# A two-layer hybrid decoder on one core: index scores of all blocks first, three selections side by side, and only the low halves of weights stored ahead

## The chip, the cores and the metric

The kernel runs on 1 core of one Trainium2 chip. Its engines are TensorE (PE, matmuls; its weight loads are listed as PEld), VectorE (DVE), ScalarE (ACT), GpSimd (POOL) and SyncE (SP, which issues most DMAs). Each works through a queue of its own in order. The metric is the device time of one execution in microseconds; lower is better.

## The reference, cut to what matters

Sequence 512, width 1024, two layers. Each layer projects the normed input once and splits it among four mixers, then does cross-attention and a gated FFN of width 2816. The change touches the second mixer, whose queries see only 256 keys each (here min(256, 512/4) = 128), chosen by an index score:

```python
def dsa_mixer(cols, pos, ...):
    ...
    topk = min(DSA_TOPK_MAX, l_ // 4)
    def block(bi):                      # 128 queries each, 4 blocks
        ...
        rel = jax.nn.relu(jnp.einsum('bthd,bsd->bhts', iqb, ik))       # 8 index heads
        score = jnp.einsum('bhts,bth->bts', rel, iwb).astype(F32)
        score = jnp.where(causal[None], score, -jnp.inf)
        _, idx = lax.top_k(score, topk)
        ...                             # attention over the chosen keys
```

The other mixers are hgrn2 (a gated linear recurrence), nsa (compressed, selected and window attention) and mlstm. The rest of a layer is `x + mixed @ w_out`, cross-attention on 256 memory rows, and `x + (silu(a) * b) @ w2` with `a, b = split(h @ w13)`.

## The kernel before

**Weights in two halves.** Matmuls keep near-float32 precision by splitting every operand into a high half (rounded by a copy) and a low half (the rest): three matmuls per product. `weight_tile` loads a raw tile (`wr`, 3 buffers; 6 in the later stages of a layer), makes the high half on ACT (`wh`, L292) and the low half on POOL (`wl`, L293); `wh` and `wl` have 6 buffers each. A typical tile is 128 x 512, 256 KB.

**Split ahead.** During layer 0's FFN, `split_ahead` does this for the 72 tiles of layer 1's first stage, in the order of the list `FIRST`: load (`pr`, 2 buffers), copy on ACT (L317), subtraction on POOL (L318), both halves written to DRAM in one transfer (`phl`, 2 buffers, L320). In layer 1 `split_tile` loads both halves from there and neither ACT nor POOL works on them. `ffn` puts `NSPLIT` = 3 such pieces into the program after each of its 22 chunks and one after every second of its 16 output columns (`fo`); the pieces left over then go into the second half's columns.

**The first stage of a layer** weaves several generators: a generator yields costs, and `mix` takes next the one that is least far along its planned total. On one side runs `dsa` (the index branch, planned total 74), then `hg_space`, which closes the index pool and opens the pool of `h_v` and `h_g` in its place. On the other side (225) run nsa's projections and its attention, mlstm's projections and its four heads, and the remaining projections (`ml_in2`, `dsa_in2`, `hg_in`). The last two of these, `hgi` and `hgg` for `h_v` and `h_g`, stand behind `hg_space`. A scheduler then orders each engine's queue at build time, by this program order and by what is ready in its own model of time; weight loads and splits are moved ahead (`first`).

**The index branch before.** For each block tb = 1, 2, 3 in turn (n = 256, 384, 512 keys; block 0 needs none): `index(tb)` splits the queries, transposes them (PE, then ACT to `iqT`), and for each of 8 heads does one matmul into one PSUM bank (`dt`), a relu on ACT (`rel`, 4 buffers) and a multiply-add into the score `iacc` on DVE. Then `select(tb)` finds the 128 largest scores of each row in 16 rounds of `max` (8 values, L696) and `match_replace` (L697; in the trace a value load and the replacement), and turns what was replaced into the mask `dmask` (L700). All blocks share one `iacc`, so the three selections run one after another.

**After the first stage** come hgrn2 with the attention of dsa and two thirds of the output projection (`hg`, `dsa_attn`, `out_stage`), then cross-attention, then the FFN. Layer 0's first stage ends near 277 us, its FFN runs from 494 to 864, layer 1's first stage from there to 1114, its FFN from 1326 to the end.

Of the kernel before, what the change touches and what calls it, by code (L numbers as in the profile page):

```python
# [21 lines left out]
NEG = -1e30  # L22
# [172 lines left out]


RAWS = 6
NSPLIT = 3

FIRST = ["dsai", "nsa0", "nsa1", "nsaT", "ml1", "mlT0", "mlT2", "cw", "ml0", "mlT1", "mlT3", "dsaq", "ckv", "hgT0", "hgT2",  # L200
         "hgT1", "hgT3", "hgi", "hgg"]
# [5 lines left out]
class Kernel:  # L207
# [73 lines left out]
    def weight_tile(self, tile, pool=None):  # L281

        nc = self.nc
        if tile in self.pre:
            return self.split_tile(tile)
        raw = self.raw_tile(tile)
        _, nk, c = tile
        kw = {"bufs": KC} if pool else {}
        hi = (pool or self.wp).tile([128, nk, c], FR, name="wh", tag="wh", **kw)
        lo = (pool or self.wp).tile([128, nk, c], FR, name="wl", tag="wl", **kw)  # L290
        with ExitStack() if pool else self.first():
            nc.scalar.activation(hi, raw, AF.Copy)  # L292
            nc.gpsimd.tensor_tensor(lo, raw, hi.bitcast(FT), op=OP.subtract)  # L293
        return [(hi[:, k], lo[:, k]) for k in range(nk)]

    def split_tile(self, tile):

        _, nk, c = tile
        both = []
        for j, n in enumerate(("wh", "wl")):  # L300
            w = self.wp.tile([128, nk, c], FR, name=n, tag=n)
            with self.first():
                self.nc.sync.dma_start(w.rearrange("p a b -> p (a b)").bitcast(FT), self.pre[tile][:, j])
            both.append(w)
        return [(both[0][:, k], both[1][:, k]) for k in range(nk)]

    def split_ahead(self, pool, l):

        nc, src = self.nc, self.i["wst"]
        for key in FIRST:  # L310
            for tile in self.plans[l][key]:
                off, nk, c = tile
                n = nk * c
                raw = pool.tile([128, n], FT, name="pr", tag="pr", bufs=2)
                nc.sync.dma_start(raw, bass.AP(tensor=src.tensor, offset=src.offset + off, ap=[[n, 128], [1, n]]))
                both = pool.tile([128, 2, n], FR, name="phl", tag="phl", bufs=2)
                nc.scalar.activation(both[:, 0], raw, AF.Copy)  # L317
                nc.gpsimd.tensor_tensor(both[:, 1], raw, both[:, 0].bitcast(FT), op=OP.subtract)  # L318
                d = self.tc.dram_tile([128, 2, n], FT, name=f"whl{off}")
                nc.sync.dma_start(d, both.bitcast(FT))  # L320
                self.pre[tile] = d
                yield

# [318 lines left out]
    def dsa(self, pool, keep):  # L642
        nc = self.nc
        idx = self.d_idx
        st = self.t(pool, "d_st", [128, 64], bufs=1)

        ik = idx[:, :, 256:288]
        self.sumsq(st[:, 4:8], ik, pool)
        self.rsqrt(pool, st[:, 8:12], st[:, 4:8], 1.0 / 32, EPS)
        self.tt(ik, ik, st[:, 8:12, None].to_broadcast([128, TB, 32]), OP.mult)  # L650
        self.tt(ik, ik, self.row("idxk_gain")[:, None, :].to_broadcast([128, TB, 32]), OP.mult)
        self.rope(idx[:, :, 256:288].rearrange("p t (h d) -> p t h d", h=1), self.ic, self.isn, 4, pool)
        iq = idx[:, :, 0:256].rearrange("p t (h d) -> p t h d", h=8)
        self.rope(iq, self.ic, self.isn, 4, pool)
        iks = self.t2(pool, "iks", [128, TB, 96], FR)
        nc.vector.tensor_copy(iks[:, :, 0:32], ik)
        nc.vector.tensor_copy(iks[:, :, 32:64], ik)
        self.tt(iks[:, :, 64:96], ik, iks[:, :, 0:32].bitcast(FT), OP.subtract)
        ikT = self.t(pool, "ikT", [128, S], FR, bufs=1)
        self.transpose_blocks(ikT[0:96], lambda j: iks[:, j, :].bitcast(FT), TB, nc.vector.tensor_copy, rows=96,  # L660
                              pool=pool)

        yield 4.0

        def index(tb):
            n = (tb + 1) * 128
            iqs = self.t(pool, "iqs", [128, 8, 96], FR, bufs=1)
            nc.scalar.activation(iqs[:, :, 0:32], iq[:, tb], AF.Copy)
            nc.scalar.activation(iqs[:, :, 64:96], iq[:, tb], AF.Copy)
            self.tt(iqs[:, :, 32:64], iq[:, tb], iqs[:, :, 0:32].bitcast(FT), OP.subtract, nc.gpsimd)  # L670
            iqT = self.t(pool, "iqT", [128, 8, 128], FR, bufs=1)
            for g in range(2):
                self.transpose_blocks(iqT[0:96, 4 * g:4 * g + 4].rearrange("p a b -> p (a b)"),
                                      lambda j: iqs[:, 4 * g + j, :].bitcast(FT), 4, self.act_copy, rows=96,
                                      pool=pool)
            acc = self.t(pool, "iacc", [128, S], bufs=1)[:, :n]
            for h in range(8):
                sc = self.psum("sc", pool=pool)
                nc.tensor.matmul(sc[:, :n], iqT[0:96, h], ikT[0:96, :n], start=True, stop=True)
                rel = self.t2(pool, "rel", [128, S])  # L680
                nc.scalar.activation(rel[:, :n], sc[:, :n], AF.Relu, scale=1.0 / 16)
                w = idx[:, tb, 288 + h:289 + h]
                if h == 0:
                    nc.vector.tensor_scalar(acc[:, :n - 128], rel[:, :n - 128], w, None, op0=OP.mult)
                    nc.vector.scalar_tensor_tensor(acc[:, n - 128:n], rel[:, n - 128:n], w, self.k("neg"),
                                                   op0=OP.mult, op1=OP.add)
                else:
                    nc.vector.scalar_tensor_tensor(acc, rel[:, :n], w, acc, op0=OP.mult, op1=OP.add)
                yield 0.7
            return acc  # L690

        def select(tb, acc, masks):
            n = (tb + 1) * 128
            m8 = self.t(pool, "m8", [128, 8])
            for r in range(16):
                nc.vector.max(m8, acc)  # L696
                nc.vector.match_replace(acc, m8, acc, -3e38)  # L697
                yield 0.4 + 0.25 * tb
            masks[tb] = self.t(keep, f"dmask{tb}", [128, n], BF, bufs=1)
            nc.vector.tensor_scalar(masks[tb], acc, -2e38, NEG, op0=OP.is_gt, op1=OP.mult)  # L700

        masks = self.d_masks = {0: None}
        for tb in range(1, TB):
            acc = yield from index(tb)
            yield from select(tb, acc, masks)

    def dsa_attn(self, pool):
        nc, l = self.nc, self.l
# [758 lines left out]
    def ffn(self, pool):  # L1467
        nc = self.nc
# [4 lines left out]
        ahead_of = lambda n: [next(ahead, None) for j in range(n)]  # L1473
        for g in range(2):
            gs = []
            for c in range(g * FFG, g * FFG + FFG):
                a = self.psum("acc")
                self.mm_T(a, self.weights(f"ffa{c}"), self.x)
                b = self.psum("sc")
# [13 lines left out]
                gs.append((gh, gl))  # L1493
                ahead_of(NSPLIT)
            for c in range(KC):
                acc = self.psum("acc")
                self.mm_T(acc, self.weights(f"fo{g}_{c}"), gs)
                if c % 2 == 0:
                    ahead_of(1)
                self.residual(c, acc)  # L1500
                if g == 1 and last_layer:
                    nc.sync.dma_start(self.o["y"][c * 128:c * 128 + 128, :], self.xT[c])
                elif g == 1:
                    self.square_sum(c)
# [32 lines left out]
    def run(self):  # L1537
        nc = self.nc
        late = ExitStack()
        for l in range(DEPTH):  # L1540
# [8 lines left out]
            right, index = ExitStack(), ExitStack()  # L1549
            self.hqf = self.pool(right, "hgqf", side="right")  # L1550
            self.mo = {2: self.t(self.mp, "mo2", [128, 2, S], bufs=1), 3: self.t(self.mp, "mo3", [128, TB, 256], bufs=1)}
            pd = self.pool(index, "dsa", n2=4, n4=0, side="right")
            self.alias[id(pd)] = {"tp": "dt", "sc": "dt"}
            acc = self.dsa_in(pd)
            if l == 0:
# [32 lines left out]
            ph = self.pool(left, "hg", n2=2, n4=0)  # L1588
# [11 lines left out]
            with ExitStack() as e:  # L1600
                p = self.pool(e, "xa")
# [29 lines left out]
```

## Time and profile before

| | us |
|---|---|
| median of 3 runs | 1687.93 |
| lowest, highest | 1684.38, 1699.76 |
| the profiled execution | 1688.9 |
| its span, first to last instruction | 1687.1 |
| its mean granted TensorE clock | 0.972 |

The profile is of one execution; times in it are microseconds from the span's start. The granted clock is given as a share of TensorE's full speed. An idle engine costs nothing unless another waits for it.

### The profile page before, as it was taken

Reading aid. Unit: us, or ns where it says so; the run is one execution under the profiler, and the core shown is the slowest. Engines: PE = TensorE matmul, PEld = TensorE weight load, DVE = VectorE, ACT = ScalarE, POOL = GpSimd, SP = SyncE. Lnnn points to the kernel's source line nnn. Section 1 sums busy time; section 2 is a strip of 40 time slices with the busy share of each in tenths; the row PEclk is TensorE's granted clock in tenths of the full one; section 3 lists DMA queues with packets and bytes.
Section 4 is the critical chain, followed back from the end, with each engine's and each line's share of the span. In section 5 each row is a group of like instructions: output and inputs, shape, how many; then the busy total and the mean of one; then the engine's idle time right before and its main releaser. Section 6 shows DMA issues by size and latency. Waiting matters only on the chain.

```text
span 1687.1 us, 25484 instructions
## 1 busy us (share of the span) xinstructions
PE 1607.5 (95%) x9256; PEld 1333.1 (79%) x9262; DVE 924.0 (55%) x1760; ACT 712.5 (42%) x1525; POOL 799.1 (47%) x698
## 2 busy tenths in 40 slices
PE   7899998998899989999999999989998999999999
PEld 7778877777788868888898887677877888888887
DVE  5697688876755330344225884879786644123420
ACT  5555453454654443443324433423665433223321
POOL 5664333456448888874412010144672344444442
PEclk9999997999999999999999999979999999999999
DMA  5342212212338999953355734122131233333331
GB/s 160 89 119 76 70 34 84 57 38 85 112 121 286 305 316 319 333 192 93 105 156 178 262 107 132 58 95 57 45 119 38 66 97 90 92 100 94 94 103 66
DMA packets 114365, 212.72 MB, mean 126 GB/s; under 512 B 12984, under 2 KB 30136, under 8 KB 114240
## 3 DMA queue, kind: packets, MB, share of 16 engines
q1 hardware_dynamic: 111888, 206.11, 38.7%
q10 hardware_dynamic: 2032, 3.94, 0.7%
q8 instruction: 73, 1.20, 0.3%
q0 software_dynamic: 320, 1.05, 0.2%
q14 instruction: 52, 0.43, 0.1%
HBM read 170.69 MB, written 40.35 MB: 125 GB/s over the span
## 4 chain that ended last, share of the span: by engine, by line
PE 84%; DVE 8%; issue 3%; DMA 2%; POOL 2%; ACT 2%; SPq 0%; POOLq 0%; ACTq 0%; DVEq 0%
PE acc L329 14%; PE acc L331 14%; PE acc L330 14%; PE sc L330 5%; PE sc L331 5%; PE sc L329 5%; PE acc L339 3%; PE acc L340 3%; PE acc L341 3%; PE hb L856 3%; PE o L574 2%; PE sc L552 2%; PE tp L493 2%; PE mb L1048 1%; PE dt L493 1%
## 5 line engine op out<-in xcount | busy, mean ns | idle before, releaser
L293 POOL TENSOR_TENSOR wl<-wr,wh 128x512 fp32r<-128x512 f32 (+5 forms) x432 | 551.7, 1285 | 459.3 <-ACT wh L292 447.8
L292 ACT ACTIVATE wh<-wr 128x512 fp32r<-128x512 f32 (+5 forms) x432 | 252.1, 592 | 336.2 <-PE acc L330 149.2
L329 PE MATMUL acc<-xh,wh 128*128 128x512 f32 (+1 forms) x704 | 276.9, 395 | 0.8 <-ACT xh L1283 0.5
L330 PE MATMUL acc<-xl,wh 128*128 128x512 f32 (+1 forms) x704 | 274.6, 390 | 2.9 <-DVE xl L1277 2.9
L331 PE MATMUL acc<-xh,wl 128*128 128x512 f32 (+1 forms) x704 | 275.4, 392 | 0.4 <-POOL wl L293 0.4
L466 DVE TENSOR_TENSOR xT<-acc,xT 128x512 f32<-128x512 f32 (+1 forms) x112 | 68.1, 611 | 214.4 <-PE acc L331 213.6
L329 PEld LDWEIGHTS acc<-xh,wh 128*128 128x128 f32 x704 | 133.9, 191 | 32.1 <-issue 1.7
L330 PEld LDWEIGHTS acc<-xl,wh 128*128 128x128 f32 x704 | 134.3, 191 | 30.8 <-DVE xl L1277 4.0
L331 PEld LDWEIGHTS acc<-xh,wl 128*128 128x128 f32 x704 | 134.1, 190 | 28.7 <-POOL wl L293 1.1
L329 PE MATMUL acc<-f_gh,wh 128*128 128x512 f32 x352 | 139.1, 397 | 6.8 <-ACT f_gh L1491 6.8
L339 PE MATMUL acc<-wh,xh 128*128 128x256 f32 (+2 forms) x480 | 140.6, 296 | 4.9 <-DMA wh<-whl 3.8
L331 PE MATMUL acc<-f_gh,wl 128*128 128x512 f32 x352 | 139.7, 398 | 0.7 <-POOL wl L293 0.7
L330 PE MATMUL sc<-xl,wh 128*128 128x512 f32 x352 | 139.7, 397 | 0.0
L330 PE MATMUL acc<-f_gl,wh 128*128 128x512 f32 x352 | 139.5, 398 | 0.0
L340 PE MATMUL acc<-wl,xh 128*128 128x256 f32 (+2 forms) x480 | 139.0, 291 | 0.0
L331 PE MATMUL sc<-xh,wl 128*128 128x512 f32 x352 | 139.0, 395 | 0.0
L329 PE MATMUL sc<-xh,wh 128*128 128x512 f32 x352 | 138.0, 393 | 0.0
L341 PE MATMUL acc<-wh,xl 128*128 128x256 f32 (+2 forms) x480 | 137.4, 288 | 0.0
L318 POOL TENSOR_TENSOR phl<-pr,phl 128x512 fp32r<-128x512 f32 (+3 forms) x72 | 95.1, 1321 | 35.0 <-ACT phl L317 31.8
L317 ACT ACTIVATE phl<-pr 128x512 fp32r<-128x512 f32 (+3 forms) x72 | 44.2, 613 | 133.9 <-DMA pr<-in_wst 117.2
L339 PEld LDWEIGHTS acc<-wh,xh 128*128 128x128 f32 x480 | 92.9, 194 | 8.8 <-DMA wh<-whl 4.3
L340 PEld LDWEIGHTS acc<-wl,xh 128*128 128x128 f32 x480 | 93.3, 195 | 1.4 <-issue 0.8
(407 smaller groups left out, 3159.8 us busy)
## 6 DMA issues: line engine op xcount, KB each, us to landing
wr<-in_wst SPq DMA_DIRECT2D x332, 256.0 KB, 2.7
whl<-phl SPq DMA_DIRECT2D x52, 512.0 KB, 3.9
pr<-in_wst SPq DMA_DIRECT2D x52, 256.0 KB, 4.1
wh<-whl SPq DMA_DIRECT2D x52, 256.0 KB, 4.1
wl<-whl SPq DMA_DIRECT2D x52, 256.0 KB, 4.4
wr<-in_wst SPq DMA_DIRECT2D x48, 128.0 KB, 2.2
wr<-in_wst SPq DMA_DIRECT2D x32, 192.0 KB, 2.4
whl<-phl SPq DMA_DIRECT2D x8, 524.0 KB, 3.7
```

The costliest lines, as they stand in the source:

```text
L292: nc.scalar.activation(hi, raw, AF.Copy)
L293: nc.gpsimd.tensor_tensor(lo, raw, hi.bitcast(FT), op=OP.subtract)
L318: nc.gpsimd.tensor_tensor(both[:, 1], raw, both[:, 0].bitcast(FT), op=OP.subtract)
L329: self.nc.tensor.matmul(acc, wh, xh, start=(j == 0), stop=False)
L330: self.nc.tensor.matmul(acc, wh, xl, start=False, stop=False)
L331: self.nc.tensor.matmul(acc, wl, xh, start=False, stop=(j == n - 1))
L339: self.nc.tensor.matmul(acc, xh[:, s], wh, start=(first and j == 0), stop=False)
L340: self.nc.tensor.matmul(acc, xh[:, s], wl, start=False, stop=False)
L341: self.nc.tensor.matmul(acc, xl[:, s], wh, start=False, stop=(last and j == n - 1))
L466: self.nc.vector.tensor_add(self.xT[c][:, cols], acc, self.xT[c][:, cols])
L493: self.nc.tensor.transpose(p[:rows, j * 128:j * 128 + 128], src(j), self.ident)
L856: nc.tensor.matmul(sc[s0:s1, b + t0:b + t1], kk[po:po + 64, b + s0:b + s1], qq[po:po + 64, b + t0:b + t1], start=True, stop=True)
```

## The change

The index scores of blocks 1 to 3 are all computed first, each into an accumulator of its own (`iacc1` to `iacc3`); queries are split and transposed four heads at a time with two buffers. Then 16 rounds run, and each round does one `max` and one `match_replace` for each of the three blocks. The masks are made at the end. Yielded costs add up to the same totals. The index pool gives one of its four `t2` buffers (among them `rel`) for this. Of the split ahead only the low half is written to DRAM (256 KB per typical tile, was 512); in layer 1 the raw tile is loaded, its high half made on ACT as in layer 0, and the low half loaded where POOL would have made it. `NSPLIT` is 2, and `ffn` puts two pieces after every chunk and every output column.

```diff
-NSPLIT = 3
+NSPLIT = 2
...
     def weight_tile(self, tile, pool=None):
-        if tile in self.pre:
-            return self.split_tile(tile)
         raw = self.raw_tile(tile)
...
             nc.scalar.activation(hi, raw, AF.Copy)
-            nc.gpsimd.tensor_tensor(lo, raw, hi.bitcast(FT), op=OP.subtract)
+            if tile in self.pre:
+                nc.sync.dma_start(lo.rearrange("p a b -> p (a b)").bitcast(FT), self.pre[tile][:, :])
+            else:
+                nc.gpsimd.tensor_tensor(lo, raw, hi.bitcast(FT), op=OP.subtract)
...
     def split_ahead(self, pool, l):
...
-                both = pool.tile([128, 2, n], FR, name="phl", tag="phl", bufs=2)
-                nc.scalar.activation(both[:, 0], raw, AF.Copy)
-                nc.gpsimd.tensor_tensor(both[:, 1], raw, both[:, 0].bitcast(FT), op=OP.subtract)
-                d = self.tc.dram_tile([128, 2, n], FT, name=f"whl{off}")
-                nc.sync.dma_start(d, both.bitcast(FT))
+                hi = pool.tile([128, n], FR, name="ph", tag="ph", bufs=2)
+                lo = pool.tile([128, n], FR, name="pl", tag="pl", bufs=2)
+                nc.scalar.activation(hi, raw, AF.Copy)
+                nc.gpsimd.tensor_tensor(lo, raw, hi.bitcast(FT), op=OP.subtract)
+                d = self.tc.dram_tile([128, n], FT, name=f"wl{off}")
+                nc.sync.dma_start(d, lo.bitcast(FT))
...
+        accs = {tb: self.t(pool, f"iacc{tb}", [128, (tb + 1) * 128], bufs=1) for tb in range(1, TB)}
...
-            iqT = self.t(pool, "iqT", [128, 8, 128], FR, bufs=1)
+                iqT = self.t(pool, "iqT", [128, 4, 128], FR, bufs=2)
...
+        for tb in range(1, TB):
+            yield from index(tb)
+
+        for r in range(16):
+            for tb in range(1, TB):
+                m8 = self.t(pool, f"m8{tb}", [128, 8])
+                nc.vector.max(m8, accs[tb])
+                nc.vector.match_replace(accs[tb], m8, accs[tb], -3e38)
                 yield 0.4 + 0.25 * tb
-            masks[tb] = self.t(keep, f"dmask{tb}", [128, n], BF, bufs=1)
-            nc.vector.tensor_scalar(masks[tb], acc, -2e38, NEG, op0=OP.is_gt, op1=OP.mult)
-
         masks = self.d_masks = {0: None}
         for tb in range(1, TB):
-            acc = yield from index(tb)
-            yield from select(tb, acc, masks)
+            masks[tb] = self.t(keep, f"dmask{tb}", [128, (tb + 1) * 128], BF, bufs=1)
+            nc.vector.tensor_scalar(masks[tb], accs[tb], -2e38, NEG, op0=OP.is_gt, op1=OP.mult)
...
                 self.mm_T(acc, self.weights(f"fo{g}_{c}"), gs)
-                if c % 2 == 0:
-                    ahead_of(1)
+                ahead_of(NSPLIT)
...
-            pd = self.pool(index, "dsa", n2=4, n4=0, side="right")
+            pd = self.pool(index, "dsa", n2=3, n4=0, side="right")
```

## Rows read from the trace of the kernel before

**Rows 1.** The page: TensorE's busy time, its busy slices and its granted clock

```profile
PE 1607.5 (95%) x9256; PEld 1333.1 (79%) x9262; DVE 924.0 (55%) x1760; ACT 712.5 (42%) x1525; POOL 799.1 (47%) x698
...
PE   7899998998899989999999999989998999999999
...
PEclk9999997999999999999999999979999999999999
```

**Rows 2.** The page: the chain that ended last, by engine

```profile
PE 84%; DVE 8%; issue 3%; DMA 2%; POOL 2%; ACT 2%; SPq 0%; POOLq 0%; ACTq 0%; DVEq 0%
```

**Rows 3.** Stretches: PE, PEld, DVE, ACT, POOL busy (instructions), clock, DMA share, GB/s

```profile
40.00:246.00 206.00, 194.59 (x1306) 162.33 (x1304) 153.34 (x318) 112.47 (x259) 100.79 (x77) 0.98 0.27 79
...
140.00:246.00 106.00, 105.72 (x664) 82.86 (x664) 76.33 (x159) 52.80 (x119) 39.26 (x30) 1.00 0.21 64
246.00:277.00 31.00, 23.09 (x129) 18.26 (x130) 28.28 (x77) 8.43 (x22) 4.52 (x6) 0.68 0.00 1
277.00:310.00 33.00, 29.22 (x204) 26.00 (x203) 27.39 (x51) 12.95 (x27) 20.34 (x25) 0.89 0.42 131
...
600.00:640.00 40.00, 32.49 (x128) 25.16 (x127) 10.56 (x12) 15.86 (x30) 34.03 (x27) 0.91 0.96 317
880.00:1080.00 200.00, 195.74 (x1339) 165.11 (x1338) 129.88 (x326) 83.16 (x205) 23.51 (x22) 0.98 0.46 155
1080.00:1114.00 34.00, 26.62 (x176) 22.44 (x174) 30.63 (x82) 11.00 (x26) 4.16 (x5) 0.80 0.00 1
```

**Rows 4.** Groups on DVE, 254.65 to 276.3 us: busy us, mean ns, idle before

```profile
L697 DVE MATCH_REPLACE8 iacc<-m,iacc 128x512 f32<-128x512 f32 x10 | 6.8, 676 | 0.0
L696 DVE MAX8 m<-iacc 128x8 f32<-128x512 f32 x9 | 6.2, 692 | 0.1
...
L697 DVE MATCH_VALUE_LOAD iacc<-m,iacc 128x8 f32 x10 | 0.9, 87 | 0.1
```

**Rows 5.** Single instructions on PE at layer 0's tail: start us, us, what

```profile
247.05 2.45 PE L1065 MATMUL mb<-m_v,m_p 128*128 128x65 f32 x20
...
254.65 0.49 PE L1048 MATMUL mb<-m_hi,m_hi 64*128 64x512 f32 x1
...
263.90 4.53 PE L1065 MATMUL mb<-m_v,m_p 128*128 128x65 f32 x20 [0.38 <-DVE m_p L1056]
```

**Rows 6.** Single instructions on DVE: the last product of mlstm in layer 0

```profile
275.87 0.42 DVE L351 TENSOR_TENSOR mo<-mo,m_tok 128x256 f32<-128x256 f32 x1
```

**Rows 7.** The tile h_v: its evacuation, ns min/median/max, first and last start

```profile
L485 ACT ACTIVATE h_v<-acc,r x8: 452/457/480, 272.8 to 1117.0; 128x256 f32<-128x256 f32 x8
```

**Rows 8.** Waits of PE, 1114 to 1141 us: total, times, longest

```profile
PE acc L339 <- DMA wh<-whl: 3.8, 1, 3.8
```

**Rows 9.** The tile iacc: its max instructions, and DVE's idle time before its instructions

```profile
L696 DVE MAX8 m<-iacc x96: 397/561/696, 79.5 to 1108.4; 128x8 f32<-128x256 f32 x32, 128x8 f32<-128x384 f32 x32, 128x8 f32<-128x512 f32 x32
...
  ACT rel L681: 35.6, 18
```

**Rows 10.** The page, groups: count, busy us, mean ns, idle before and its releaser

```profile
L329 PE MATMUL acc<-f_gh,wh 128*128 128x512 f32 x352 | 139.1, 397 | 6.8 <-ACT f_gh L1491 6.8
...
L318 POOL TENSOR_TENSOR phl<-pr,phl 128x512 fp32r<-128x512 f32 (+3 forms) x72 | 95.1, 1321 | 35.0 <-ACT phl L317 31.8
L317 ACT ACTIVATE phl<-pr 128x512 fp32r<-128x512 f32 (+3 forms) x72 | 44.2, 613 | 133.9 <-DMA pr<-in_wst 117.2
```

**Rows 11.** The whole run's DMA issues: count, KB each, median us to landing

```profile
whl<-phl SPq DMA_DIRECT2D x52, 512.0 KB, 3.9
pr<-in_wst SPq DMA_DIRECT2D x52, 256.0 KB, 4.1
...
whl<-phl SPq DMA_DIRECT2D x8, 296.0 KB, 2.7
```

**Rows 12.** The subtractions of L318 in two stretches: POOL busy (instructions), clock, DMA, GB/s

```profile
640.00:660.00 20.00, 7.82 (x6) 1.00 0.95 315
740.00:760.00 20.00, 0.00 (x0) 1.00 0.38 109
```

More of the change, by code (lines that the diff above doesn't have):

```diff
@@ L292, in weight_tile @@
             nc.scalar.activation(hi, raw, AF.Copy)
-            nc.gpsimd.tensor_tensor(lo, raw, hi.bitcast(FT), op=OP.subtract)
+            if tile in self.pre:
+                nc.sync.dma_start(lo.rearrange("p a b -> p (a b)").bitcast(FT), self.pre[tile][:, :])
+            else:
+                nc.gpsimd.tensor_tensor(lo, raw, hi.bitcast(FT), op=OP.subtract)
         return [(hi[:, k], lo[:, k]) for k in range(nk)]
[L296 to L305, printed above, removed]
     def split_ahead(self, pool, l):
@@ L663, in dsa @@
         yield 4.0
+        accs = {tb: self.t(pool, f"iacc{tb}", [128, (tb + 1) * 128], bufs=1) for tb in range(1, TB)}
         def index(tb):
             n = (tb + 1) * 128
[L667 to L670, printed above, removed]
-            iqT = self.t(pool, "iqT", [128, 8, 128], FR, bufs=1)
@@ L672, in index @@
-            for g in range(2):
[L673 to L697, printed above, removed]
+            acc = accs[tb]
+            for g in range(2):
+                four = iq[:, tb, 4 * g:4 * g + 4]
+                iqs = self.t(pool, "iqs", [128, 4, 96], FR, bufs=1)
+                nc.scalar.activation(iqs[:, :, 0:32], four, AF.Copy)
+                nc.scalar.activation(iqs[:, :, 64:96], four, AF.Copy)
+                self.tt(iqs[:, :, 32:64], four, iqs[:, :, 0:32].bitcast(FT), OP.subtract, nc.gpsimd)
+                iqT = self.t(pool, "iqT", [128, 4, 128], FR, bufs=2)
+                self.transpose_blocks(iqT[0:96].rearrange("p a b -> p (a b)"), lambda j: iqs[:, j, :].bitcast(FT), 4,
+                                      self.act_copy, rows=96, pool=pool)
+                for h in range(4 * g, 4 * g + 4):
+                    sc = self.psum("sc", pool=pool)
+                    nc.tensor.matmul(sc[:, :n], iqT[0:96, h % 4], ikT[0:96, :n], start=True, stop=True)
+                    rel = self.t2(pool, "rel", [128, S])
+                    nc.scalar.activation(rel[:, :n], sc[:, :n], AF.Relu, scale=1.0 / 16)
+                    w = idx[:, tb, 288 + h:289 + h]
+                    if h == 0:
+                        nc.vector.tensor_scalar(acc[:, :n - 128], rel[:, :n - 128], w, None, op0=OP.mult)
+                        nc.vector.scalar_tensor_tensor(acc[:, n - 128:n], rel[:, n - 128:n], w, self.k("neg"),
+                                                       op0=OP.mult, op1=OP.add)
+                    else:
+                        nc.vector.scalar_tensor_tensor(acc, rel[:, :n], w, acc, op0=OP.mult, op1=OP.add)
+                    yield 0.7
```

## The prediction

> **What bounds the kernel now.** I read the page's busy table and slices first, then one table of stretches, then the groups, waits and single instructions of the stretches where something else than TensorE set the time. TensorE (PE) is busy 95% of the span, and its slices dip in few places; the granted clock dips in two slices, the 7th (253 to 295 us) and the 27th (1097 to 1139), the ends of the two layers' first stages [rows 1]. The chain that ended last is 84% PE and only 8% VectorE (DVE) [rows 2]. So time can be won only where PE stands idle or runs at the lower of its two levels (1.2 of 2.4 GHz), and what fills other engines under a full PE is free.
>
> Three such places matter here [rows 3]. From 246 to 277 us (end of layer 0's first stage) PE is busy 23.1 of 31 us at a mean granted clock of 0.68: at full clock that work is 23.1 x 0.68 = 15.7 us, so 15.3 us are lost, while DVE is busy 28.3. From 1080 to 1114 (the same place in layer 1) it is 26.6 x 0.80 = 21.3 us of work in 34, 12.7 lost, DVE busy 30.6. From 600 to 640 (layer 0's FFN) PE idles 7.5 us, and its 32.5 busy us at 0.91 hold 2.9 more: 10.4 lost, with the DMA engines busy at 0.96. Together 38 us, the whole that the change could aim at.
>
> **The selections.** In the 21.6 us from the first score matmul of mlstm's last head [rows 5] to its last product on DVE [rows 6], DVE runs ten replace and nine max instructions of the third selection with ten value loads: 6.8 + 6.2 + 0.9 = 13.9 us [rows 4]. Every one is a step of a single dependent chain, started late: its eight index heads come only after the second selection, although DVE had 53 idle us between 40 and 246 [rows 3]. The head's own short DVE steps queue between them, PE waits for these, and its clock falls: the 20 value matmuls of this head take 4.53 us, those of the head before 2.45 [rows 5]. Meanwhile gate and value projections of hgrn2 (hgi, hgg) stand: the evacuation of hgi first runs at 272.8 us [rows 7], since h_v lies in the space of the index pool, which is released after the last selection.
>
> The change removes no selection work and adds none; it moves 16 of 24 index heads per layer ahead of all rounds and lets three chains of rounds run from then on. They become filler for DVE's idle time under a full PE (140 to 246 us), so I expect the last round well before mlstm's end. What is late next is mlstm's last head alone. Bounds for layer 0: at the least its chain loses two thirds of the 13.9 us, since steps of other work stay between (9); at the most all 15.3 come back, with hgi and hgg filling PE. I take 10.5, nearer to the chain, because the chain and not PE's work ends the stage. Layer 1 has 12.7 to lose and the same chain: 10.5 too. There PE also waits 3.8 us for a weight load just behind the tail [rows 8]; DMA moves 1 GB/s in the tail because hgi's unread weights hold buffers [rows 3]. I count 2 of it (0 to 3.8). Sum: **-23**.
>
> What it gives back behind the tail: hgi and hgg now cover the start of the next stage, 277 to 310 us. Moved into the tail, they cover it no longer. That start is DVE's more than PE's (27.4 of 33 us busy, PE 29.2 at 0.89 [rows 3]), and it begins earlier with the tail's end; so I take 1.5 per layer for a PE that is slower there (0 to all of the 10.5). Sum: **+3**.
>
> What the index heads cost in the first third: DVE waited 35.6 us in all for the relu outputs of ScalarE (ACT), in 18 cases of the 48 heads, 0.74 per head [rows 9]. 16 heads per layer move into a stretch in which PE does idle (11.4 us between 40 and 246, 4.3 in layer 1's 880 to 1080 [rows 3]), with one PSUM bank for their transposes and scores as before and three buffers for relu instead of four. At worst all 16 x 0.74 = 12 us per layer land on PE. Against it, the rounds of the first selection leave that stretch (16 max and 16 replace, from 0.4 us each [rows 9]: 13 us of DVE), and PE gets the heads' matmuls where it idled; so it can be a gain of some 5. I take +1 per layer, near the middle. Who waits behind a late relu on DVE: nsa's key preparation and through it its scores. Sum: **+2**.
>
> **The stored splits.** Each of 72 pieces kept a high and a low half (512 KB out); now only the low half goes out, 256 KB. The write took 3.9 us at 512 KB and 2.7 at 296 [rows 11], so a 256 KB write takes between 2.0 (half) and 2.7; it is not awaited. The 72 subtractions on GpSimd (POOL, 1.32 us each) and copies on ACT (0.61) stay [rows 10]. DMA writes fall by 72 x 0.25 = 18 MB; the reads are equal, since layer 1 loads the raw tile where it loaded the high half.
>
> The FFN loss is one stop: PE waited 6.8 us for f_gh on ACT [rows 10], and ACT stood before copies of pieces for their loads (117 us in all [rows 10]), loads that took 4.1 us [rows 11] on full DMA engines. The third of the pieces' traffic that goes should shorten these loads, and buffers of the high half come free without the write. I take -7 of the 10.4 (0 to 10.4): the stop, without its clock. But the new spacing (two pieces per chunk and two per output column, before three and a half) may do little: at 640 to 660 us, where the program order gives one piece per two output columns, 6 run in 20 us, and by 740 all are done [rows 12], long before the last columns. The pieces run ahead of their place already, paced by their two buffers. Sum: **-7**.
>
> One rule of the Trainium skill speaks against the halved write: "DMA: Bandwidth & Descriptors", section Bandwidth, says to batch transfers to 1 MiB or more, because smaller ones reach less of the peak. From its table (0.95 us at 64 KB, 6.15 at 1 MB, a line between them) I estimate that a 256 KB write takes 0.59 of a 512 KB one, so that 41% of the write would be saved and not half, the FFN term would be 0.82 x 7 = 5.7, and the time 1668.
>
> Layer 1 pays: 72 copies of 0.61 us = 44 us on ACT, for halves that came by DMA before. ACT was busy 83 of 200 us in layer 1's first stage; it would be near 127. Layer 0's stage ran with 112 of 206 on ACT and POOL splitting as well, and there PE idled 11.4 us against 4.3 [rows 3]: 7.1 for both engines together, the nearest row. ACT is half of that: **+3** (0 to 7.1; to 44 if nothing hides it). Raw loads have three buffers where the halves had six each; SP's queue issues two loads per tile as before, and a raw load that waits for its buffer holds the low half's behind it; in layer 0 the same three buffers serve.
>
> The profiled execution took 1688.9 us (span 1687.1), the median is 1687.93, so the sum carries over within 1: -23 + 3 + 2 - 7 + 3 = -22, **1667 us**, own range 1657 to 1678.
>
> **The rivals.**
> First, all comes back: PE stays full through both tails (-15.3 - 12.7 - 3.8), the FFN stop goes whole (-10.4) and nothing is paid: -42, 1647. For it: PE was full from 140 to 246 [rows 3], so early heads also take matmuls out of that. Against it: the start of the next stage is DVE's.
> Second, moved and not won: the start of the next stage finds PE uncovered and gives back all 23: 1688.9 + 2 - 7 + 3 = 1687. For it: hgi and hgg made PE's work there; against it: that start's own chain begins earlier.
> Third, the spacing does not do what it says: pieces run ahead as before, and ACT stops f_gh again: 1667 + 7 = 1674.
> Fourth, slower: ACT's in-order queue in layer 1. If none of the 44 us is hidden, relus, exponentials and evacuations of index, nsa and mlstm stand behind copies that wait for raw loads, and PE behind these: 1667 + 41 = 1708. It turns the change into a loss once more than 25 of the 44 us (57%) show. Against it: ACT had 117 idle us there.
>
> **How the numbers follow.** Chances: forecast 0.48, first rival 0.16, second 0.15, third 0.09, fourth 0.12. About 1% (17 us; the three runs spread by 0.9%) is what a measurement tells here: faster means below 1671. Of the forecast's 0.48 two thirds lie there (0.32), all of the first rival (0.16) and half of the third (0.05): 0.53. Above 1705 lies most of the fourth: 0.10. The rest, 0.37, is no change. The range reaches from 1648, the first rival's edge, to 1690, past the second, and leaves out the fourth and half of the first.
>
> **What would show it.** Right: the last max instruction of layer 0 lies well before the last mo product, hgi's evacuation is in one run before it, and the stretch that ends the first stage shows a clock near 1 with PE busy. Max and replace of three widths alternate from the first third on. In the FFN the wait for f_gh is gone or small and DMA stands nearer 0.8 than 0.96. In layer 1 ACT gains some 44 us, with PE's idle time there up by a few us. Wrong: DVE still saturated at the stage's end (rounds left over), PE idle moved to the first 40 us of the next stage, new PE waits for relu or exp in 60 to 110 us or behind wh copies at 880 to 1000, or POOL so full of pieces that wl comes late.

## The result, and the profile after

The changed kernel takes 1709.8 us (median of 4 runs, 1707.45 to 1711.14), the kernel before 1686.66 (4 runs by now). The ratio is 1.0132, interval 1.0105 to 1.0159: 1.3% slower, where 1667 us and a gain of 1.2% were forecast. The profiled execution took 1710.1 us (span 1708.3), 21.2 more than that of before. In e2_select, e6_serial and e9_pipe_bank below one run was slow, at a lower granted clock; medians count it, ratios leave it out.

The page of the changed kernel: TensorE's busy time, its slices and its clock, against [rows 1].

```profile
PE 1614.1 (94%) x9256; PEld 1333.0 (78%) x9262; DVE 908.2 (53%) x1760; ACT 756.3 (44%) x1609; POOL 799.4 (47%) x704
...
PE   7888999899899989999999799998998999999999
...
PEclk9987999999999999999999789999999999999999
```

The two dips of the clock are still two, but earlier: they were in slices 7 and 27, the ends of the two first stages, and are now in slices 3 and 4 (85 to 171 us) and 23 and 24 (940 to 1025), in the middle of those stages. Stretches of the changed kernel, columns as in [rows 3]:

```profile
40.00:246.00 206.00, 182.76 (x1187) 151.02 (x1186) 144.87 (x342) 106.44 (x245) 90.00 (x72) 0.91 0.27 75
...
246.00:277.00 31.00, 31.00 (x232) 26.07 (x231) 14.67 (x23) 16.98 (x37) 15.75 (x12) 1.00 0.19 51
277.00:310.00 33.00, 30.19 (x189) 25.38 (x189) 16.36 (x43) 11.50 (x25) 12.84 (x18) 0.95 0.28 87
600.00:640.00 40.00, 31.97 (x129) 24.82 (x129) 14.57 (x16) 18.08 (x33) 35.35 (x27) 0.91 0.81 262
880.00:1080.00 200.00, 184.88 (x1236) 154.96 (x1235) 134.02 (x353) 106.46 (x252) 22.05 (x23) 0.92 0.48 153
1080.00:1114.00 34.00, 34.00 (x234) 27.73 (x232) 15.46 (x28) 16.41 (x35) 5.76 (x4) 1.00 0.26 78
120.00:140.00 20.00, 8.39 (x25) 4.87 (x25) 19.92 (x42) 9.61 (x19) 6.27 (x4) 0.52 0.09 27
960.00:1000.00 40.00, 27.47 (x119) 17.97 (x119) 39.85 (x98) 21.44 (x51) 6.89 (x7) 0.62 0.12 41
```

Busy time times clock is the work that PE did, in full-clock us. The old tails are full now: 246 to 277 went from 15.7 to 31.0 (+15.3), 1080 to 1114 from 21.3 to 34.0 (+12.7). That is not yet a gain, since the stretches ahead of them lost more: 40 to 246 went from 194.59 x 0.98 = 190.7 to 182.76 x 0.91 = 166.3 (-24.4), 880 to 1080 from 195.74 x 0.98 = 191.8 to 184.88 x 0.92 = 170.1 (-21.7). The clock is given to two places, so each of these is good to about 1 us. The holes lie at 120 to 140 us, where PE is busy 8.4 of 20 us at a clock of 0.52, and at 960 to 1000; there DVE is full (19.92 of 20) and DMA nearly idle.

Who waited there: waits of PE from 40 to 280 us in the changed kernel (total, times, longest).

```profile
PE dt L673 <- ACT rel L675: 6.6, 6, 1.9
PE tp L512 <- DVE n_hs L342: 4.7, 1, 4.7
PE mb L484 <- DVE m_g L342: 4.3, 1, 4.3
...
PE dt L1192 <- ACT rel L675: 0.7, 1, 0.7
```

L673 is the index product. L1192 transposes `n_hid`, a step of nsa's compression; that it waits for `rel`, a tile of the index, is the clue. Both use the PSUM bank `dt`. The tile `dt` from 40 to 200 us, before and after (count, ns min/median/max, first and last start):

```profile
L679 PE MATMUL dt<-ikT,iqT x16: 279/310/687, 51.1 to 145.5; 96*128 96x256 f32 x8, 96*128 96x384 f32 x8
...
L1200 PE MATMUL dt<-kc,n_hid x4: 222/248/275, 104.3 to 149.4; 64*128 64x64 f32 x4
```

```profile
L673 PE MATMUL dt<-ikT,iqT x24: 280/430/795, 47.3 to 131.4; 96*128 96x256 f32 x8, 96*128 96x384 f32 x8, 96*128 96x512 f32 x8
...
L1192 PE MATMUL dt<-kc,n_hid x4: 214/270/367, 132.9 to 155.8; 64*128 64x64 f32 x4
```

Before, nsa's transposes ran at 104.3 us, between the first head of block 2 (83.8) and its second (115.8). After, all 24 heads run first, the last at 131.4, and the transposes follow at 132.9, though ACT writes their input from 104.3 us on (102.0 before):

```profile
L1189 ACT ACTIVATE n_hid<-acc x2: 363/364/366, 104.3 to 153.9; 64x256 f32<-64x256 f32 x2
```

What the forecast said of the tail did come: the masks are done at 186 us, the evacuation of hgi is in the tail [rows 7], and the last head's 20 value matmuls take 2.45 us where they took 4.53 [rows 5]. But mlstm's last product, at 275.87 before [rows 6], runs at 303.63 (in layer 1 at 1148.1, before at 1113.6): the first stage itself now ends some 28 and 34 us later, and part of what fills the old tails is work that came late. The rounds did not alternate in three widths from the first third on, as was expected: in layer 0 the 16 of block 1 ran by themselves from 82 to 112 us, and those of blocks 2 and 3 alternate from 140. The scheduler orders them by its own model of time. The tiles `dmask`, `h_v` and `mo` of the changed kernel:

```profile
L697 DVE TENSOR_SCALAR dmask<-iacc x3: 279/427/952, 114.0 to 186.2; 128x256 bf16<-128x256 f32 x1, 128x384 bf16<-128x384 f32 x1, 128x512 bf16<-128x512 f32 x1
```

```profile
L476 ACT ACTIVATE h_v<-acc,r x8: 465/474/476, 261.7 to 1120.8; 128x256 f32<-128x256 f32 x8
```

```profile
L342 DVE TENSOR_TENSOR mo<-mo,m_tok x4: 412/413/1408, 210.5 to 303.6; 128x256 f32<-128x256 f32 x4
```

The FFN of layer 0, groups of the page and DMA issues, against [rows 10, 11]:

```profile
L320 PE MATMUL acc<-f_gh,wh 128*128 128x512 f32 x352 | 138.9, 397 | 8.0 <-ACT f_gh L1483 8.0
...
L308 ACT ACTIVATE ph<-pr 128x512 fp32r<-128x512 f32 (+3 forms) x72 | 44.2, 614 | 113.3 <-DMA pr<-in_wst 107.4
```

```profile
pr<-in_wst SPq DMA_DIRECT2D x52, 256.0 KB, 3.0
wl<-pl SPq DMA_DIRECT2D x52, 256.0 KB, 2.7
```

Loads take 3.0 us (4.1 before), DMA is busy 0.81 (0.96), and the stop is still there: 8.0 us, before 6.8.

### The profile page after: what moved, and what is told of

Same layout as the page of the kernel before. It is cut to its first block, busy times and chain, and to the rows that moved or that the text cites. A ratio compares the mean times of both kernels' runs of the same rounds, so it can differ in the third digit from the quotient of the medians.

```text
span 1708.3 us, 25647 instructions
## 1 busy us (share of the span) xinstructions
PE 1614.1 (94%) x9256; PEld 1333.0 (78%) x9262; DVE 908.2 (53%) x1760; ACT 756.3 (44%) x1609; POOL 799.4 (47%) x704
## 4 chain that ended last, share of the span: by engine, by line
PE 78%; DVE 8%; DMA 2%; issue 1%; ACT 1%; POOL 1%; SPq 0%; DVEq 0%; ACTq 0%; POOLq 0%
PE acc L320 13%; PE acc L321 13%; PE acc L322 13%; PE sc L321 5%; PE sc L322 5%; PE sc L320 5%; PE acc L330 3%; PE acc L331 3%; PE acc L332 3%; PE o L565 2%; PE tp L484 2%; PE hb L848 2%; PE sc L543 2%; PE mb L1040 1%; PE mb L1057 1%
## 5 line engine op out<-in xcount | busy, mean ns | idle before, releaser
L294 POOL TENSOR_TENSOR wl<-wr,wh 128x512 fp32r<-128x512 f32 (+5 forms) x432 | 543.5, 1266 | 508.8 <-ACT wh L290 490.2
L290 ACT ACTIVATE wh<-wr 128x512 fp32r<-128x512 f32 (+5 forms) x504 | 297.2, 595 | 425.3 <-PE acc L321 170.5
L309 POOL TENSOR_TENSOR pl<-pr,ph 128x512 fp32r<-128x512 f32 (+3 forms) x72 | 94.4, 1311 | 21.4 <-ACT ph L308 19.6
L308 ACT ACTIVATE ph<-pr 128x512 fp32r<-128x512 f32 (+3 forms) x72 | 44.2, 614 | 113.3 <-DMA pr<-in_wst 107.4
```

## The experiments

**Theory.** Tiles of the one-buffer bank `dt` are handed out in program order, and the change puts 24 heads in a row there. Each head is a round trip (product on PE, relu on ACT), so nsa's compression, next in line for `dt`, comes some 30 us late, and PE runs out of work. **Rivals:** the 72 copies that ACT gained in layer 1; the rounds of three selections that fill DVE.

Each run below is of 5 rounds beside the kernel before on the same chip; ratios are to that.

### Which half of the change

**e1_storage**: the kernel before with `weight_tile`, `split_ahead`, `ffn` and `NSPLIT` of the change.

```diff
-NSPLIT = 3
+NSPLIT = 2
...
-                both = pool.tile([128, 2, n], FR, name="phl", tag="phl", bufs=2)
+                hi = pool.tile([128, n], FR, name="ph", tag="ph", bufs=2)
+                lo = pool.tile([128, n], FR, name="pl", tag="pl", bufs=2)
```

> The change's storage and spacing alone (low halves stored, two pieces per chunk and per output column), with the index branch of the kernel before. Theory (the index heads crowd the one PSUM bank dt and push nsa's compression back): storage is nearly free, within 4 us of the kernel before, 1683 to 1691. Rival one (ACT's 72 added copies make layer 1 slow): layer 1's first two stages lost 15 us where layer 0's lost 7, so the copies cost some 8: 1695. The stop of f_gh in layer 0's FFN stays at 6 to 8 us in either.

Measured: 1692.5 us, ratio 1.0025 (1.0006 to 1.0043): +4 us, between the theory's range and the 1695 of rival one.

**e2_select**: the kernel before with the index branch of the change.

```diff
-            acc = yield from index(tb)
-            yield from select(tb, acc, masks)
+        for tb in range(1, TB):
+            yield from index(tb)
+        for r in range(16):
+            for tb in range(1, TB):
```

> The change's index branch alone (all heads first, three selections side by side, three t2 buffers), with the storage and spacing of the kernel before. Theory, and rival two (rounds of three selections saturate DVE): nearly the whole loss is here, 1704 to 1710, with PE's gap at 120 to 140 us as in the changed kernel. Rival one (ACT copies): only twice layer 0's 7 us, 1699 to 1702.

Measured: 1706.9 us, 1.0101 (1.0074 to 1.0127): +17 by the ratio. The halves add up (1.0126 against 1.0132). Most of the loss is the index branch's; ACT's copies, which e2_select lacks, are not the cause of that part.

### Bank or DVE

**e3_bank**: the changed kernel, and in `nsa_cmp`:

```diff
-            p = self.psum("dt", (128, 2, 64))
+            p = self.psum("mb", (128, 2, 64))
...
-            p = self.psum("dt", (128, 64))
+            p = self.psum("mb", (128, 64))
```

> The changed kernel with one difference: the first two uses of the bank dt by nsa's compression (transposes of n_hid, product with n_hT) go to the bank mb, so they no longer stand behind the 24 index heads. Theory: the transposes run near 105 us, as in the kernel before, the gap of PE at 120 to 140 us (and 960 to 1000) mostly goes, 6 to 10 us per layer: 1690 to 1698. Rival two (DVE saturated by the rounds): the transposes run early but what follows them waits for DVE; within 4 us of the changed kernel, 1706 to 1713.

Measured: 1668.0 us, 0.9873 (0.9838 to 0.9908): 42 us less than the changed kernel, more than the theory asked for, and faster than the kernel before. **e14_bank_again**, the same kernel on another chip:

> The kernel of e3_bank once more, beside the two runs with the subtraction on DVE: it should repeat its ratio to the kernel before, 0.984 to 0.991.

Measured: 1672.3 us, 0.9904 (0.9873 to 0.9936), 38 us less than the changed kernel. Stretches of e3_bank:

```profile
120.00:140.00 20.00, 18.98 (x163) 16.87 (x161) 19.93 (x39) 12.07 (x30) 11.43 (x8) 1.00 0.46 132
960.00:1000.00 40.00, 40.00 (x269) 33.45 (x268) 36.35 (x85) 22.99 (x50) 5.84 (x7) 1.00 0.43 128
246.00:277.00 31.00, 30.48 (x245) 25.87 (x243) 8.73 (x23) 16.02 (x37) 11.37 (x10) 1.00 0.18 52
1080.00:1114.00 34.00, 30.15 (x219) 24.53 (x219) 23.30 (x50) 15.47 (x33) 15.85 (x22) 1.00 0.31 96
40.00:246.00 206.00, 195.03 (x1300) 164.69 (x1300) 167.54 (x357) 112.31 (x264) 102.04 (x79) 0.96 0.28 79
880.00:1080.00 200.00, 197.45 (x1382) 168.38 (x1381) 144.67 (x362) 115.79 (x273) 24.83 (x25) 1.00 0.49 157
```

The transposes of `n_hid` run from 107.8 us. At 120 to 140 us DVE is as full as in the changed kernel (19.93) and PE is busy 18.98 at full clock. So a full DVE did not make the hole. From 40 to 246 us PE does 195.03 x 0.96 = 187.2 us of work (before 190.7, changed 166.3), from 880 to 1080 197.4 (191.8, 170.1). The old tails hold 30.5 and 30.2 us, 14.8 and 8.9 more than before: 23.7, where 23 was forecast. The bank is not all that differs from the changed kernel: the scheduler orders everything anew after an edit, and in e3_bank the rounds of blocks 2 and 3 no longer alternate. They did so only from 140 us on (986 in layer 1), when the hole was already there.

**e11_heads_mb**: the changed kernel, with the index in `mb`.

```diff
-            self.alias[id(pd)] = {"tp": "dt", "sc": "dt"}
+            self.alias[id(pd)] = {"tp": "mb", "sc": "mb"}
```

> The changed kernel with its index transposes and scores in the bank mb, where mlstm works, instead of dt; nsa's compression keeps dt. Theory (whoever shares the heads' bank waits for the last head): n_hid's transposes run near 105 us again, but mlstm's gate transposes, at 80 to 112 us in the changed kernel, move behind the heads, so the loss turns up with mlstm: 1680 to 1700, between e3_bank and the changed kernel. Rival (nsa's compression alone is what PE lacked): as e3_bank, 1664 to 1672. Rival two (the bank is not the cause but a better order that came by chance with mb): 1705 to 1713.

Measured: 1703.2 us, 1.0074 (1.0047 to 1.0100), a little above the theory's range. The transposes of `n_hid` run from 107.1 us, and mlstm's gate transposes, in the changed kernel from 80.4, stand behind the heads; tile `mb` of e11_heads_mb, then of e3_bank:

```profile
L673 PE MATMUL mb<-ikT,iqT x24: 280/394/690, 48.5 to 160.1; 96*128 96x256 f32 x8, 96*128 96x384 f32 x8, 96*128 96x512 f32 x8
L484 PEld LDWEIGHTS mb<-kc,m_g x8: 81/85/86, 162.1 to 164.6; 128*4 128x4 f32 x8
```

```profile
L484 PEld LDWEIGHTS mb<-kc,m_g x8: 82/84/85, 120.9 to 124.1; 128*4 128x4 f32 x8
```

Whoever shares the heads' bank waits for the last head. Neither bank is better as such; in `mb`, mlstm pays: its last product comes at 298.1 us, and from 277 to 310 us PE does 27.94 x 0.69 = 19.3 us of work where it did 26.0 before. A wait for a bank need not cost time, though: in e3_bank the same gate transposes run at 120.9 us, behind nsa's compression, and PE has other work meanwhile.

**e5_bank_alone**: the kernel before with the edit of e3_bank.

> The kernel before with the bank change alone (nsa's compression takes mb instead of dt for its first two uses). Theory (the bank costs only when all heads stand in one row): in the kernel before the transposes of n_hid ran at once, so nothing is won, 1682 to 1691. Rival (the bank was crowded all along, and the changed kernel with it gone merely shows that): a gain of 8 or more, below 1680.

Measured: 1680.6 us, 0.9955 (0.9937 to 0.9973): -7, just below the theory's range and just above the rival's bound. So a third or more of what e3_bank wins over the kernel before is the bank's alone, and the bank was somewhat crowded before. Edit by edit: by the ratios the index branch of the change costs 17 us with the crowded bank and, with it freed, gains 11 (0.9955 to 0.9891, e7_best below).

### Order of heads and rounds, and storage, with the bank free

**e6_serial**: e3_bank, rounds one block after another.

```diff
-        for r in range(16):
-            for tb in range(1, TB):
+        for tb in range(1, TB):
+            for r in range(16):
```

> The run e3_bank with the rounds of the three selections one block after another again (all heads still first, three accumulators). Theory: the rounds' work on DVE is the same and has time until mlstm's last head in either order, so within 5 us of e3_bank, 1663 to 1673. Rival one (only side by side keeps the selections off the end): the last selection ends late again and 6 to 10 us come back, 1674 or more. Rival two (side by side floods DVE at 100 to 200 us): undoing it gains, below 1662.

Measured: 1670.5 us, 0.9890 (0.9856 to 0.9925), within the theory's range. But the run does not test the order of the rounds. In e3_bank, too, DVE ran the three selections one after another, although the program writes them side by side: the scheduler gave both kernels the same order of instructions on DVE in the first stages. The last `max` of block 2 and the first of block 3, in e3_bank and in e6_serial:

```profile
168.57 0.56 DVE L691 MAX8 m<-iacc 128x8 f32<-128x384 f32 x1
171.23 0.68 DVE L691 MAX8 m<-iacc 128x8 f32<-128x512 f32 x1
```

```profile
167.91 0.56 DVE L691 MAX8 m<-iacc 128x8 f32<-128x384 f32 x1
170.57 0.68 DVE L691 MAX8 m<-iacc 128x8 f32<-128x512 f32 x1
```

So the gain of e3_bank does not come from selections side by side; whether these would gain or lose with the bank free is open.

**e4_pipe**: e2_select with the heads of block tb+1 between the rounds of block tb. **e9_pipe_bank**: the same with the bank edit.

```diff
+        yield from index(1)
+        for tb in range(1, TB):
+            if tb < TB - 1:
+                yield from self.mix((rounds(tb), 16 * (0.4 + 0.25 * tb)), (index(tb + 1), 5.6))
+            else:
+                yield from rounds(tb)
+            mask(tb)
```

> Storage as in the kernel before; the index branch with three accumulators, but block tb+1's heads between the rounds of block tb (two rounds per head) rather than all heads first and three selections side by side. Theory: heads are spread out again, nsa's compression isn't pushed back, and the last selection starts earlier than before by its eight heads: 1670 to 1682, with the clock dip at 246 to 277 us shorter. Rival two: with at most one chain of rounds at a time DVE isn't saturated either, so it gives the same; what it tells apart is the loss from the gain: if the tail's 15 us come back and PE is still slower later, a rival of its own (the work hgi and hgg did behind the tail is missing) gives 1684 to 1690.

> The run e4_pipe (block tb+1's heads between the rounds of block tb, storage as before) with the bank change. Theory (the bank is what cost; the order of heads and rounds matters little once it is free): a gain of 25 to 30 us on e4_pipe, equal to e7_best within 4 us, 1664 to 1672. Rival (heads spread out are better for DVE's queue too): below 1662.

Measured: 1695.1 us, 1.0043 (1.0018 to 1.0069), and 1675.7, 0.9941 (0.9915 to 0.9966). Spreading the heads out, where I expected a gain, loses too: the transposes of `n_hid` start at 115.9 us in e4_pipe, 12 later than before, as more heads still come ahead of them (14, before 9). That is not the whole: PE's work from 40 to 246 us falls by 6 us, but behind the old tails (277 to 480 and 1114 to 1148) by 14, which fits the rival of the missing cover without showing it. The bank edit gains 17 by the ratios, less than expected, and e9_pipe_bank lies above its range: with the bank free, spread heads gain half of what e7_best gains with all heads first.

**e7_best**: e2_select with the bank edit, so the storage of before.

> The changed index branch with the bank change, and the storage and spacing of the kernel before (both halves stored). Storage alone cost 4 us: 1661 to 1666 if the parts add. If ACT's added copies cost more in a stage where PE is fuller, 1655 to 1660; if they were free there, 1666 to 1670.

Measured: 1668.1 us, 0.9891 (0.9863 to 0.9918). It is not better than e3_bank: with the bank free the storage, and with it ACT's copies, costs nothing that shows.

### The stop in layer 0's FFN

**e8_loads**: e3_bank, four load buffers, the low half written in place.

```diff
-                raw = pool.tile([128, n], FT, name="pr", tag="pr", bufs=2)
+                raw = pool.tile([128, n], FT, name="pr", tag="pr", bufs=4)
...
-                lo = pool.tile([128, n], FR, name="pl", tag="pl", bufs=2)
+                lo = raw.bitcast(FR)
```

> The run e3_bank with four load buffers per piece of the split ahead instead of two (the low half is written in place, so the space is the same). Theory of the FFN's stop: each copy on ACT waits 1.6 to 2 us for its load because only two loads are under way, and f_th and f_gh of the half's last chunk stand behind four such copies; with four the loads have landed, and the 7 us wait of PE for f_gh goes: 1658 to 1663. Rival (POOL, busy 18 of 20 us, or the DMA engines set the pieces' pace): copies then wait for POOL instead and the stop stays, 1666 to 1670.

Measured: 1702.2 us, 1.0080 (1.0051 to 1.0108). A miss for the theory as I put it: copies waited for loads longer than before (118.9 us from 480 to 740, in e3_bank 100.0), and waits of PE for `wl` came on top. PE was busy 234.24 of the 260 us, in e3_bank 252.03. Why the loads came so late is open.

**e10_chunk**: e3_bank, in `ffn` the first chunk of the second half ahead of the first half's output columns.

```diff
+        last = []
         for g in range(2):
-            gs = []
-            for c in range(g * FFG, g * FFG + FFG):
+            gs = last
+            for c in range(g * (FFG + 1), NFF if g else FFG + 1):
...
+            last = gs[FFG:]
...
-                self.mm_T(acc, self.weights(f"fo{g}_{c}"), gs)
+                self.mm_T(acc, self.weights(f"fo{g}_{c}"), gs[:FFG])
```

> The run e3_bank with one change in the FFN: the first chunk of the second half stands before the first half's output columns, so PE has some 8 us of work while f_th and f_gh of the first half's last chunk stand behind copies on ACT. Theory (the stop is a matter of ACT's queue order at this one place, not of the pieces' pace): the wait of PE for f_gh goes with its clock dip, 7 to 10 us: 1657 to 1662. Rival (the pace of the split ahead sets the FFN's time, so the stop turns up at another place): 1665 to 1670.

Measured: 1677.6 us, 0.9913 (0.9884 to 0.9942): no gain. **e12_chunk_dve** is e10_chunk, **e13_dve** is e3_bank, both with the pieces' subtraction on DVE:

```diff
-                nc.gpsimd.tensor_tensor(lo, raw, hi.bitcast(FT), op=OP.subtract)
+                nc.vector.tensor_tensor(lo, raw, hi.bitcast(FT), op=OP.subtract)
```

> The run e10_chunk with the pieces' subtraction on DVE instead of GpSimd. In e10_chunk PE's wait for f_gh was gone, and waits for wl of GpSimd had come in its place. Theory (two limits lie one behind the other: ACT's queue at the turn of the halves, then GpSimd, busy 17 to 19 of 20 us): with both gone the FFN of layer 0 takes some 368 us as layer 1's does, 7 to 9 less than in e3_bank: 1658 to 1663. Rival (DVE's in-order queue then stands behind the pieces as GpSimd's did): no gain, 1667 to 1680.

> The run e3_bank with the pieces' subtraction on DVE alone, the order of the chunks as in the changed kernel. Theory: GpSimd was not what stopped PE there, so ACT's copies still stand before f_gh and the 7 us stay: within 4 us of e3_bank. Rival (GpSimd's pace makes the copies wait): the stop shrinks to below 3 us.

Measured: 1674.7 us, 0.9914 (0.9880 to 0.9948), and 1672.0, 0.9917 (0.9877 to 0.9956): no gain either. The longest waits of PE from 480 to 740 us in e10_chunk, e12_chunk_dve and e13_dve, where e3_bank waits 7.3 for f_gh:

```profile
PE acc L322 <- POOL wl L294: 5.7, 8, 1.3
```

```profile
PE acc L320 <- DVE xT L457: 4.7, 3, 2.6
PE acc L320 <- DVE f_a L1475: 3.8, 1, 3.8
```

```profile
PE acc L320 <- DVE f_a L1474: 3.8, 1, 3.8
PE acc L320 <- DVE xT L457: 2.2, 5, 0.9
PE acc L320 <- ACT f_gh L1483: 1.6, 1, 1.6
```

The wait for f_gh shrinks to 1.6 us in e13_dve, as its rival had it, but in sum PE still loses 7.4 to 8.6 us in this stretch: take the stop from one engine and another makes it. What these have in common is a piece's instruction that waits in an in-order queue with work for PE behind it. That points at the pieces' pace, but does not show it.

**e15_pace**: e3_bank, load buffers and `f_th` in one ring of four. **e16_pace_chunk**: the same with the edit of e10_chunk.

```diff
-                raw = pool.tile([128, n], FT, name="pr", tag="pr", bufs=2)
+                raw = pool.tile([128, 528], FT, name="pr", tag="pr", bufs=4)[:, :n]
...
-                th = self.t(pool, "f_th", [128, S], bufs=2)
+                th = pool.tile([128, 528], FT, name="f_th", tag="pr", bufs=4)[:, :S]
```

> The run e3_bank with the pieces of the split ahead held to their place: their load buffers and the chunks' f_th share one ring of four, so a piece's load cannot start before the f_th of the chunk before it is used (two pieces in each chunk's 8 us instead of one every 3 us). Theory (pieces that run ahead put copies that wait for loads into ACT's queue before f_th and f_gh): with the pace held, PE's idle time in layer 0's FFN, 8 us in each variant so far, falls below 2: 1657 to 1663 by e3_bank's profiled 1664 or its median 1668 to 1672 less 8. Rival (each piece costs its share of PE's time wherever it stands): 7 to 9 us stay, 1664 to 1672.

> The run e15_pace with the first chunk of the second half ahead of the first half's output columns, as in e10_chunk. Theory: nothing is left to hide there, so it equals e15_pace within 3 us. Rival: a stop at the turn of the halves is left in e15_pace and goes here, 4 or more us.

Measured: 1662.5 us, 0.9847 (0.9813 to 0.9881), and 1662.2, 0.9850 (0.9817 to 0.9883). The stretch 480 to 740 us in e3_bank and in e15_pace:

```profile
480.00:740.00 260.00, 252.03 (x1084) 203.30 (x1083) 91.33 (x98) 111.08 (x196) 215.65 (x163) 0.99 0.73 227
```

```profile
480.00:740.00 260.00, 260.00 (x1131) 210.92 (x1130) 98.02 (x109) 110.35 (x186) 192.58 (x145) 1.00 0.59 189
```

PE's 8 idle us are gone, DMA falls from 0.73 to 0.59, and ACT's waits for `pr` from 100.0 us to 7.2. The theory holds: the pace was the cause of the stop. That the ring has four buffers is not enough: e8_loads had four without the tie to `f_th`, if with the low half in place, and lost. e16_pace_chunk adds nothing. These two are the fastest kernels of the study, 1.5% below the kernel before; their gain over e3_bank (0.9873, and 0.9904 again) is not clear of the intervals.

## Why the prediction was wrong

**The step that failed** is "What the index heads cost in the first third". It took +1 us per layer and set the worst case at 16 x 0.74 = 12 by counting one thing, DVE's wait for relu [rows 9]. Measured in full-clock work, the two stretches lost 24.4 and 21.7; with the bank freed, in e3_bank, they lose 3.5 and gain 5.6. The relief that it counted against the heads, the first selection's 13 us of DVE leaving the stretch, did not come either: those rounds run from 82 to 112 us, as before (79.5 to 111.8). The text named "one PSUM bank for their transposes and scores as before" and didn't ask who else uses it. As for who waits, it named nsa's key preparation, by way of DVE; it was nsa's compression, by way of the bank. e3_bank shows the cause by taking it away, e11_heads_mb by moving it to mlstm. The Trainium skill has the rule in "Perfetto Trace Analysis", section Matmuls: independent groups of matmuls should go through different PSUM banks, so that the evacuation of one lies beside the matmuls of the next. e3_bank agrees, with 42 us (38 in e14_bank_again), for two groups of different mixers.

**The tails** (-23) were right in mechanism: the masks are done early, and hgi and hgg run before mlstm ends. The changed kernel can't give their size. Its 15.3 and 12.7 us more, the upper bounds of the estimates, are in part work that came late; e3_bank gives 23.7. The +3 given back behind the tails can't be read at 277 to 310 us (30.19 x 0.95 = 28.7 of work where it held 26.0 [rows 3]), since in the changed kernel that is still the end of the first stage.

**The FFN** (-7) measured nothing (the stop is 8.0 us, was 6.8). The third rival had it right: pieces run ahead of their place, paced by two buffers, and `NSPLIT` does not hold them. Its sign [rows 12] was before me and I priced the loads' duration instead. e15_pace got the 8 us by holding the pace.

**The storage in layer 1** (+3) was not measured by itself. e1_storage has +4 for storage, copies and FFN together, where the forecast had -7 + 3 = -4; with the bank free (e7_best against e3_bank) none of it shows. The 256 KB write was put between 2.0 and 2.7 us and took 2.7. By the Trainium skill, "DMA: Bandwidth & Descriptors", section Bandwidth, I had estimated a write of 0.59 of the 512 KB one's time (the table there is of loads); the medians give 2.7 / 3.9 = 0.69, so even less was saved than that page's table let expect. It decided nothing.

**The fourth rival**, the one slower case, was of the right sign for the wrong reason: ACT's queue in layer 1. e2_select has none of its copies and 17 us of the loss.

**The sum** by rows: +28.0 in the tails, +2.7 behind the first, -46.1 ahead of them, and in the FFN's stretch 32.49 x 0.91 = 29.6 against 31.97 x 0.91 = 29.1, -0.5. That makes a loss of 15.9 of the 21.2 measured. Two more stretches lost work: 310 to 480 us (159.50 x 0.96 = 153.1, then 155.67 x 0.96 = 149.4, -3.7) and 1114 to 1326 (200.06 x 0.96 = 192.1, then 196.61 x 0.95 = 186.8, -5.3); with them it is 24.9, which the rounding of the clock can bring to 21.2. All of it lies ahead of layer 1's FFN, whose `f_a` is first written at 1357.2 us, before at 1335.9. With the first term's cause removed the forecast's 1667 is what e3_bank measured, though in part by luck: a bank gain that nobody forecast (7 us by e5_bank_alone) stands in it for the FFN gain of 7 that did not come.

## What to carry to other kernels

When work is moved ahead, list every shared tile, bank and buffer that it passes on its way, and ask who stands next in line for each: with one buffer, the order of the program is the order of use, whatever is ready. A long row of round trips belongs in a bank that nobody else wants at that time. Filler work that is paced only by its own buffers runs ahead until it blocks an in-order queue; to move the blocking instruction to another engine moves the stop, and a true dependence on the main work removes it.

## What the runs showed of the hardware that was not expected

The same stop can cost very different time through the clock. In e3_bank and e15_pace PE comes to 320 us with nearly the same work and idles there for 1.9 of 4 us in both. The clock then falls to its lower level, 1.2 of 2.4 GHz. Stretches of 4 us, first e3_bank, then e15_pace:

```profile
320.00:324.00 4.00, 2.09 (x18) 1.77 (x15) 4.00 (x12) 1.51 (x8) 0.87 (x2) 0.95 0.00 0
324.00:328.00 4.00, 4.00 (x22) 3.59 (x21) 2.96 (x9) 1.44 (x5) 1.42 (x2) 0.50 0.01 2
328.00:332.00 4.00, 4.00 (x27) 3.47 (x27) 3.97 (x12) 0.60 (x1) 1.78 (x3) 0.70 0.01 4
332.00:336.00 4.00, 3.60 (x36) 2.95 (x36) 4.00 (x9) 1.90 (x6) 1.47 (x2) 1.00 0.00 0
```

```profile
320.00:324.00 4.00, 2.09 (x19) 1.90 (x17) 4.00 (x9) 1.50 (x8) 0.73 (x1) 0.90 0.01 1
324.00:328.00 4.00, 4.00 (x21) 3.36 (x21) 2.75 (x10) 1.41 (x5) 0.70 (x2) 0.50 0.01 2
...
344.00:348.00 4.00, 4.00 (x18) 3.22 (x16) 1.86 (x6) 1.86 (x5) 1.54 (x3) 0.50 0.10 33
348.00:352.00 4.00, 4.00 (x25) 3.54 (x26) 1.47 (x3) 0.90 (x2) 0.66 (x1) 0.68 0.14 33
```

In e3_bank the clock is back at 332 us, in e15_pace only after 348, though PE was busy all that time. From 320 to 360 us that is 37.69 x 0.91 = 34.3 us of work against 38.09 x 0.66 = 25.1, a difference of 9 us. It takes up what the FFN of e15_pace won: the two profiled executions are level (spans 1662.5 and 1661.9), with differences of up to 6 us either way in other stretches. Runs of one and the same kernel spread with the clock, too: the six of e3_bank go from 1657.8 us at a mean clock of 0.986 to 1678.8 at 0.971, and the faster of any two has the higher clock. What decides how long the clock stays low there was not tried and is left open.
